# A 32-byte pad moved ahead of the attention tiles, and 64 bytes left free at the right end of SBUF, in a float32 encoder layer

## The chip, the core and the metric

One NeuronCore of a Trainium2 chip runs one launch of the kernel. The metric is the device time of that launch in microseconds (us). Engines are named as in the profile: PE (TensorE matmuls) and PEld (TensorE's weight loads), DVE (VectorE), ACT (ScalarE), POOL (GpSimd) and SP (SyncE, which issues all DMAs here). SBUF, the on-chip memory, has 128 partitions; a tile takes the same range of bytes in each of them, and an "address" below is the byte at which a tile starts within a partition.

## What is computed

One encoder layer over 2048 rows of width 1024, all in float32, cut from the reference:

```python
h = x * (1.0 + sc1) + sh1                        # sc, sh, g from the conditioning vector
proj = jnp.einsum('bsd,de->bse', h, w_in[l])     # u (512 wide) and q, k, v (512 each)
y_pool = pool_mixer(u, w_pool[l], pool_scale[l])         # means over 2/4/8/16 rows
y_attn = chunked_attention(q, k, v, rel_bias[l])         # 64-row chunks, 9-chunk band, 8 heads
y = jnp.einsum('bse,ed->bsd', jnp.concatenate([y_pool, y_attn], axis=-1), w_out[l])
x = layer_norm(ALPHA * x + (1.0 + g1) * y, ln1_g[l], ln1_b[l])
h = x * (1.0 + sc2) + sh2
f = jnp.square(jax.nn.relu(jnp.einsum('bsd,df->bsf', h, w_ff1[l])))    # 1024 -> 4096
f = jnp.einsum('bsf,fd->bsd', f, w_ff2[l])                             # 4096 -> 1024
x = layer_norm(ALPHA * x + (1.0 + g2) * f, ln2_g[l], ln2_b[l])
```

## The kernel before

Every large product is done in split float32: an operand is cut into a high part in the matmul format float32r and the rest, a low part, and three matmuls (high x high, high x low, low x high) stand for one. A matmul here has two SBUF operands: 128x128 *weights*, which are loaded first, and a *moving* operand of, mostly, 128 partitions by 512 columns of 4 bytes, which is streamed past them.

The stages, in order of time:

- **First projections** (lines 154 to 229, about 0 to 55 us): `wf` holds the weights, `hT` the modulated input, which is moving (L172).
- **Attention** (lines 231 to 750, about 55 to 640 us): `step` issues the other projections (L441, weights from `hl`, moving `hT`) a few matmuls at a time between the attention matmuls of one of 128 units: scores S (L623, weights `q`, moving `k`), transposes T of the probabilities `s` (L646) and values (L667, weights `v`, moving `PT`). DVE, ACT and POOL do the softmax and the splits.
- **Output projection** (`wout_half`, L402, weights `hl`, moving `hT`), layer norm and its transposes (L841), about 640 to 841 us.
- **Up projection** (`product`, L1067, about 841 to 1480 us): 32 turns `g`, each of seven products `s` of 12 matmuls; the weights come from `hl`, the moving operand from `hslot[s]`. The slots 0, 1, 2 and 5 are tiles of the pool `sa` (printed as `h` in the trace, `f<-h,hl`), the slots 3, 4 and 6 are tiles `sb` of the pool `big` (`f<-sb,hl`).
- **Down projection** (`f2_products` and `issue`, L1351, from about 1494 us): weights from `sa` tiles, moving `sb` tiles, 2688 matmuls, then the last layer norm.

The program's order is written out by hand: each engine runs its instructions in the order in which the code issues them, with semaphore waits between engines. What the change touches is where tiles lie. A pool takes its room in the order in which pools are opened, from the left end of SBUF upwards or, with `side="right"`, from the right end downwards, and a closed pool's room is used again by the next one. On the left stand, in this order, constants and small tiles, `stream` (`raw`, `hl`), then the first projections' pool `ada`, in its place later `attn`, and in their place, after `attnp.__exit__` at line 753, a pool `pad` of 32 bytes (lines 754 and 755) and behind it `sa` and the rest. On the right stands `big` alone: four tiles of 16384 bytes, first `hT`, later `sb` and `g`. The memset of a pad only makes the tile exist; nobody reads it.

Of the kernel before, what the change touches and what calls it, by code (L numbers as in the profile page):

```python
# [8 lines left out]
F32 = mybir.dt.float32  # L9
# [15 lines left out]
def trunk_layer(ctx: ExitStack, tc: tile.TileContext, xT, x, wada1, wada2, vecs, rows, win, wfirst, wpT, wout,  # L25
                bias, w1, w2, out):
    nc = tc.nc
# [86 lines left out]
            a_items[hf, name] = st.add(win[where[name[0]] + int(name[1])], nc.gpsimd)  # L114

    late = {}
    yi = [st.add(yS[t // 8][t % 8].rearrange("p k c -> p (k c)"), nc.vector) for t in range(16)]
    big = ctx.enter_context(tc.tile_pool(name="big", bufs=1, side="right"))
    hTs = [big.tile([128, 2, 2, 1024], F32R, name="hT", tag="big", bufs=4) for _ in range(4)]
# [24 lines left out]
    def narrow(w=512):  # L144
        return pr.tile([128, w], F32, name="pv", tag="pv", bufs=1)

    adap = tc.tile_pool(name="ada", bufs=1)
    ada = adap.__enter__()
    NF0 = len(FIRST)
# [601 lines left out]


    attnp.__exit__(None, None, None)
    padp = ctx.enter_context(tc.tile_pool(name="pad", bufs=1))
    nc.gpsimd.memset(padp.tile([128, 8], F32, name="pad"), 0.0)
    sap = ctx.enter_context(tc.tile_pool(name="sa", bufs=1))

    def slot(i, name):
# [707 lines left out]
```

## Time and profile before

| what | us |
|---|---|
| median of 3 runs | 2108.86 |
| the 3 runs | 2104.95, 2108.86, 2114.11 |
| the profiled execution, its own time | 2109.24 |
| its span, first to last instruction | 2107.5 |
| PE busy in the span | 2039.2 |
| DVE busy | 1311.7 |
| ACT busy | 1000.1 |
| POOL busy | 322.8 |

The profile is of one execution. Its timeline gives the start of a run of like instructions, the time to the end of the last one, and their count; since matmuls overlap, the time from one start to the next, divided by the count, is the pitch at which they follow each other, and this is shorter than the mean duration that a list of groups gives for one matmul.

### The profile page before, as it was taken

What the parts mean: (1) busy time and instruction counts of PE and PEld (TensorE: products, weight loads), DVE (VectorE), ACT (ScalarE), POOL (GpSimd) and SP (SyncE); (2) the same over time, 40 slices, a digit from 0 to 9 for tenths busy, and PEclk for the clock granted to TensorE, in tenths of its full rate; (3) what the DMA queues carried; (4) which work ended last, traced back from release to release, by engine and by line L of the source; (5) the groups of instructions that cost most, each with busy time, mean ns of one, the idle gap of its engine ahead of it and who ended that gap; (6) DMA issues with size and microseconds to landing.
All of it is one profiled execution on the core that took longest, in us unless ns stands there. A gap on an engine that the chain in (4) does not pass through costs nothing.

```text
span 2107.5 us, 27049 instructions
## 1 busy us (share of the span) xinstructions
PE 2039.2 (97%) x9672; PEld 1682.2 (80%) x9672; DVE 1311.7 (62%) x1974; ACT 1000.1 (47%) x1592; POOL 322.8 (15%) x426
## 2 busy tenths in 40 slices
PE   7999989999999999999999999999999999999998
PEld 6778868887877888778888788888788888888886
DVE  7555566556665464777766766666694447875448
ACT  5454555554553555545545655555453333333330
POOL 1535443553333100000000000000000001100002
PEclk9999999999999999999999999999999999999999
DMA  7444553434433678879878988887986556766552
GB/s 300 139 136 127 148 156 99 137 107 137 135 123 105 200 240 296 290 254 322 293 266 295 322 278 292 300 295 274 326 287 209 190 190 210 255 236 227 191 170 110
DMA packets 210360, 456.68 MB, mean 217 GB/s; under 512 B 18609, under 2 KB 36529, under 8 KB 209202
## 3 DMA queue, kind: packets, MB, share of 16 engines
q1 hardware_dynamic: 210226, 454.96, 64.1%
q8 instruction: 76, 1.25, 0.2%
q14 instruction: 58, 0.48, 0.1%
HBM read 294.45 MB, written 152.05 MB: 212 GB/s over the span
## 4 chain that ended last, share of the span: by engine, by line
PE 82%; DVE 7%; ACT 4%; DMA 3%; issue 2%; POOL 1%; SPq 0%; DVEq 0%; POOLq 0%; ACTq 0%
PE f L1351 26%; PE f L1067 26%; PE d L441 10%; PE d L402 7%; PE pv L667 3%; PE T L646 3%; PE S L623 2%; DVE s L630 1%; ACT PT L654 1%; PE d L172 1%; DVE PT L655 1%; PE S L172 1%; ACT s L632 1%; ACT hl L59 1%; DVE sb L60 1%
## 5 line engine op out<-in xcount | busy, mean ns | idle before, releaser
L1351 PE MATMUL f<-sb,sa 128*128 128x512 f32 x2688 | 616.3, 391 | 2.5 <-DVE sb L60 1.8
L1351 PEld LDWEIGHTS f<-sb,sa 128*128 128x128 f32 x2688 | 504.7, 188 | 114.0 <-DVE sb L60 2.5
L441 PE MATMUL d<-hT,hl 128*128 128x512 f32 x1392 | 373.2, 400 | 0.7 <-ACT vt L333 0.7
L1067 PE MATMUL f<-h,hl 128*128 128x512 f32 x1536 | 363.5, 392 | 3.5 <-ACT c L1074 2.7
L1067 PEld LDWEIGHTS f<-h,hl 128*128 128x128 f32 x1536 | 288.2, 188 | 69.7 <-ACT c L1074 4.0
L1067 PE MATMUL f<-sb,hl 128*128 128x512 f32 x1152 | 280.8, 397 | 8.0 <-ACT c L1074 5.1
L441 PEld LDWEIGHTS d<-hT,hl 128*128 128x128 f32 x1392 | 248.7, 189 | 41.0 <-ACT vt L333 1.1
L1067 PEld LDWEIGHTS f<-sb,hl 128*128 128x128 f32 x1152 | 218.5, 190 | 59.9 <-ACT c L1074 6.2
L655 DVE TENSOR_TENSOR PT<-T,PT 128x640 fp32r<-128x640 f32 (+4 forms) x128 | 94.8, 741 | 211.3 <-ACT PT L654 209.3
L632 ACT ACTIVATE s<-s,m 128x640 f32<-128x640 f32 (+4 forms) x128 | 97.9, 765 | 236.7 <-DVE m L630 182.6
L402 PE MATMUL d<-hT,hl 128*128 128x512 f32 x696 | 166.0, 395 | 0.0
L1089 ACT ACTIVATE g<-g 128x512 f32<-128x512 f32 x96 | 60.7, 633 | 213.9 <-DVE g L1080 213.9
L59 ACT CAST sb<-hl 128x1024 fp32r<-128x1024 f32 x67 | 70.2, 1048 | 178.4 <-PE f L1351 153.1
L402 PEld LDWEIGHTS d<-hT,hl 128*128 128x128 f32 x696 | 129.3, 189 | 27.0
L638 POOL TENSOR_SCALAR s<-s,m 128x640 f32<-128x640 f32 (+4 forms) x128 | 99.3, 776 | 253.2 <-DVE m L637 214.0
L60 DVE TENSOR_TENSOR hl<-wsum,hl 128x1024 fp32r<-128x1024 f32 x64 | 78.4, 1225 | 93.6 <-ACT hl L59 93.6
L60 DVE TENSOR_TENSOR sb<-hl,sb 128x1024 fp32r<-128x1024 f32 x67 | 81.9, 1222 | 68.8 <-ACT sb L59 68.5
L59 ACT CAST sb<-raw 128x1024 fp32r<-128x1024 f32 x53 | 55.3, 1052 | 119.0 <-PE f L1351 94.8
L623 PE MATMUL S<-k,q 128*128 128x320 f32 (+1 forms) x448 | 91.9, 321 | 16.6 <-DVE m L630 16.6
L623 PEld LDWEIGHTS S<-k,q 128*128 128x128 f32 x448 | 74.4, 188 | 36.3 <-DVE m L630 22.8
L1394 POOL TENSOR_SCALAR ag<-ag 128x1024 f32<-128x1024 f32 x1 | 1.0, 1047 | 665.3 <-DMA ab<-in_rows_dram 665.3
L60 DVE TENSOR_TENSOR hl<-w,hl 128x1024 fp32r<-128x1024 f32 x64 | 61.3, 957 | 63.3 <-ACT hl L59 63.3
(182 smaller groups left out, 2613.1 us busy)
## 6 DMA issues: line engine op xcount, KB each, us to landing
fS<-g SPq DMA_DIRECT2D x224, 256.0 KB, 4.2
hl<-fS SPq DMA_DIRECT2D x67, 512.0 KB, 4.6
hl<-tS SPq DMA_DIRECT2D x67, 512.0 KB, 4.9
w<-in_w_dram SPq DMA_DIRECT2D x48, 512.0 KB, 4.3
raw<-fS SPq DMA_DIRECT2D x45, 512.0 KB, 4.5
raw<-tS SPq DMA_DIRECT2D x45, 512.0 KB, 4.8
wS<-wsum SPq DMA_DIRECT2D x32, 512.0 KB, 4.8
raw<-in_w_dram SPq DMA_DIRECT2D x32, 512.0 KB, 5.1
```

The lines of the kernel that those rows point to most:

```text
L59: nc.scalar.copy(hl_h, src)
L60: low.tensor_sub(hl_l, src, hl_h.bitcast(F32))
L402: nc.tensor.matmul(ps, yc[:, a, k, :], hT(b, k, cols), start=(k == 0 and i == 0), stop=(k == 7 and i == 2))
L441: nc.tensor.matmul(ps, w[name][:, a, k, :], hT(b, k, slice(tb * 512, tb * 512 + 512)), start=(n == 0), stop=(n == 23))
L623: nc.tensor.matmul(S[:, 512 * p:512 * p + wp], q[:, i * 128:i * 128 + 128], k[:, a, k0 + p * wp:k0 + p * wp + wp], start=(a == 0), stop=(a ...
L632: nc.scalar.activation(s[:, 0:w], s[:, 0:w], AF.Exp, bias=m[:, 0:1], scale=-1.0, accum_out=m[:, 1:2])
L638: nc.gpsimd.tensor_scalar(s[:, 0:nk * 128], s[:, 0:nk * 128], m[:, 1:2], 1.0, op0=ALU.mult, op1=ALU.mult)
L646: nc.tensor.transpose(t[:, j * 128:j * 128 + 128], s[:, j * 128:j * 128 + 128], ident)
L655: nc.vector.tensor_sub(ol, src, oh.bitcast(F32))
L667: nc.tensor.matmul(pv, v[:, i + sl, h % 2, :], PTt[:, a, sl, :], start=(c == 0), stop=(c == tot - 1))
L1067: nc.tensor.matmul(ps, w[:, p, c:c + 128], h[:, q, k, :], start=first and k == 0 and (p, q) == (0, 0), stop=k == 3 and p == 1, skip_group_ ...
L1351: nc.tensor.matmul(bank, f, w, start=start, stop=stop, skip_group_check=True)
```

## The change

The pad pool is opened before `ada`, and so also before `attn`, and stays open; it is no longer opened after `attn`. A second pool of 64 bytes is opened on the right ahead of `big`.

```diff
     late = {}
+    padr = ctx.enter_context(tc.tile_pool(name="padr", bufs=1, side="right"))
+    nc.gpsimd.memset(padr.tile([128, 16], F32, name="padr"), 0.0)
...
     def narrow(w=512):
         return pr.tile([128, w], F32, name="pv", tag="pv", bufs=1)
 
+
+    pad = ctx.enter_context(tc.tile_pool(name="pad", bufs=1))
+    nc.gpsimd.memset(pad.tile([128, 8], F32, name="pad"), 0.0)
     adap = tc.tile_pool(name="ada", bufs=1)
...
     attnp.__exit__(None, None, None)
-    padp = ctx.enter_context(tc.tile_pool(name="pad", bufs=1))
-    nc.gpsimd.memset(padp.tile([128, 8], F32, name="pad"), 0.0)
     sap = ctx.enter_context(tc.tile_pool(name="sa", bufs=1))
```

The addresses that the pools then give, and what remains of them after division by 256. The slices of the matmul operands start at multiples of 512 bytes within their tiles, so a slice has its tile's remainder; where a pool holds several such tiles, all have the same one.

| tile | use | address before | remainder before | address after | remainder after |
|---|---|---|---|---|---|
| `hl` (first of 3) | weights L441, L402, L1067 | 10656 | 160 | 10656 | 160 |
| `sa` (first of 4) | moving L1067, weights L1351 | 35744 | 160 | 35744 | 160 |
| `hT`, `sb` (first of 4) | moving L172, L441, L402, L1067, L1351 | 163808 | 224 | 163744 | 160 |
| `wf` | weights L172 | 35712 | 128 | 35744 | 160 |
| `q` / `k` | weights / moving L623 | 61056 / 69248 | 128 / 128 | 61088 / 69280 | 160 / 160 |
| `v` / `PT` | weights / moving L667 | 36480 / 93824 | 128 / 128 | 36512 / 93856 | 160 / 160 |
| `xr` | DMA target, ACT and DVE operand | 129856 | 64 | 129888 | 96 |
| `xk` | DMA target, ACT and DVE operand | 93056 | 128 | 93088 | 160 |
| `raw` | DMA target, ACT and DVE operand | 2464 | 160 | 2464 | 160 |

No other instruction is added, removed or moved, on any engine, and the waits between engines are the same but for those of the pad. POOL at the start of the program, before and after (`ident` and `mhalf` are constants, the last row is the split of the first streamed weights):

```order
 masks.py:197 MEMSET ident 128x128
 masks.py:199 ISA
 masks.py:199 AFFINE_SELECT ident<-ident 128x128
 L51 MEMSET mhalf 128x1
+L118 MEMSET padr 128x16
+L151 MEMSET pad 128x8
 L60 TENSOR_TENSOR hl<-raw,hl 128x512 x4
```

Two memsets now stand between the last constant and POOL's first split. POOL at the end of attention, before:

```order
L356 TENSOR_TENSOR ws_6431<-u 128x527
L356 TENSOR_TENSOR ws_6432<-ws_6431 128x525
L638 TENSOR_SCALAR s<-s,m 128x640 x2
L755 MEMSET pad 128x8
L795 TENSOR_SCALAR mv<-mv 128x1
```

In the changed program the memset of `pad` is gone from this place, between the last softmax work and the first layer-norm work.

## Rows read from the trace of the kernel before

**Rows 1.** The page's chain that ended last, by engine and by line, shares of the span.
```profile
PE 82%; DVE 7%; ACT 4%; DMA 3%; issue 2%; POOL 1%; SPq 0%; DVEq 0%; POOLq 0%; ACTq 0%
PE f L1351 26%; PE f L1067 26%; PE d L441 10%; PE d L402 7%; PE pv L667 3%; PE T L646 3%; PE S L623 2%; DVE s L630 1%; ACT PT L654 1%; PE d L172 1%; DVE PT L655 1%; PE S L172 1%; ACT s L632 1%; ACT hl L59 1%; DVE sb L60 1%
```
**Rows 2.** Windows: PE, PEld, DVE, ACT, POOL busy (count), clock, DMA share, GB/s.
```profile
0.00:50.00 50.00, 38.19 (x183) 32.35 (x184) 37.02 (x92) 26.35 (x30) 4.38 (x10) 1.00 0.78 306
...
50.00:640.00 590.00, 559.26 (x3144) 472.13 (x3143) 342.29 (x758) 307.62 (x629) 256.42 (x322) 0.99 0.45 133
...
1000.00:1480.00 480.00, 475.66 (x2070) 387.87 (x2069) 316.61 (x399) 259.03 (x384) 0.00 (x0) 1.00 0.83 289
1500.00:2040.00 540.00, 540.00 (x2361) 443.05 (x2360) 338.56 (x324) 208.75 (x204) 16.72 (x18) 1.00 0.67 228
```
**Rows 3.** Timeline of PE, one up-projection turn: start, us to last end, count.
```profile
1209.91 8.37 PE L1067 MATMUL f<-h,hl 128*128 128x512 f32 x36
1218.12 5.67 PE L1067 MATMUL f<-sb,hl 128*128 128x512 f32 x24
1223.63 2.93 PE L1067 MATMUL f<-h,hl 128*128 128x512 f32 x12
1226.40 2.93 PE L1067 MATMUL f<-sb,hl 128*128 128x512 f32 x12
1229.16 3.16 PE L1067 MATMUL f<-h,hl 128*128 128x512 f32 x13
```
**Rows 4.** The same timeline asked from 1213.0 on: the last 24 of those 36.
```profile
1212.68 5.60 PE L1067 MATMUL f<-h,hl 128*128 128x512 f32 x24
```
**Rows 5.** PE in two windows of that turn: busy, clock, DMA share, GB/s.
```profile
1212.70:1218.10 5.40, 5.40 (x25) 1.00 0.98 356
1218.10:1223.60 5.50, 5.50 (x25) 1.00 0.82 257
```
**Rows 6.** Timeline of PE in the down projection, 1500 to 1600 us.
```profile
1499.80 100.42 PE L1351 MATMUL f<-sb,sa 128*128 128x512 f32 x438
```
**Rows 7.** Pieces of the chain that ended last (start, us): values, output projection.
```profile
379.39 1.43 PE pv L667 x12
...
702.07 11.01 PE d L402 x48
```
**Rows 8.** Timeline of PE in the first projections.
```profile
27.72 0.86 PE L172 MATMUL d<-hT,wf 128*128 128x512 f32 x3
28.42 0.39 PE L172 MATMUL pv<-hT,wf 128*128 128x512 f32 x1
28.66 0.63 PE L172 MATMUL S<-hT,wf 128*128 128x512 f32 x2
...
30.52 0.86 PE L172 MATMUL d<-hT,wf 128*128 128x512 f32 x3
```
**Rows 9.** Timeline of PE in attention.
```profile
386.08 1.55 PE L441 MATMUL d<-hT,hl 128*128 128x512 f32 x6
387.46 0.71 PE L646 MATMUL T<-ident,s 128*128 128x128 f32 x5
```
**Rows 10.** Groups by line and shape: count, busy us, mean ns of one, idle before.
```profile
L441 PE MATMUL d<-hT,hl 128*128 128x512 f32 x1392 | 373.2, 400 | 0.7 <-ACT vt L333 0.7
...
L667 PE MATMUL pv<-PT,v 128*128 128x256 f32 x672 | 97.2, 292 | 0.1
...
L623 PE MATMUL S<-k,q 128*128 128x320 f32 x384 | 74.2, 315 | 9.9 <-DVE m L630 9.8
...
L59 ACT CAST hl<-raw 128x512 fp32r<-128x512 f32 x90 | 53.5, 615 | 9.6 <-PE S L402 9.5
...
L59 ACT CAST hT<-xr 128x512 fp32r<-128x512 f32 x16 | 9.5, 615 | 0.0
```
**Rows 11.** Timeline of POOL at the start.
```profile
1.24 0.10 POOL L51 MEMSET mhalf<- 128x1 f32 x1
46.35 4.60 POOL L60 TENSOR_TENSOR hl<-raw,hl 128x512 fp32r<-128x512 f32 x3 [45.02 <-ACT hl L59]
```

## The prediction

> **What bounds the kernel now.** I read the chain that ended last first, then windows by stage, then PE's timeline inside the long stages. PE holds 82% of the chain, and its lines there are the large products, L1351 and L1067 with 26% each, L441 with 10%, L402 with 7% [rows 1]. The windows say the same by stage: PE is busy for 475.66 of 480 us in the up projection and for all of 540 in the down projection, while DVE, the next engine, has 317 and 339, and the DMA engines stand at 0.83 and 0.67 [rows 2]. So there the time is the number of matmuls times their pitch, the time from one start to the next. Nothing waits, and nothing is removed by this change; whatever it does to the total it must do through the pitch, or through the price of other operations whose tiles now lie elsewhere.
>
> The pitch is not the same everywhere, though the shape is. In one turn of the up projection the 24 matmuls from 1212.68 on take until 1218.12 us, 226.7 ns each; the next 24 take until 1223.63, 229.6 ns each [rows 3, 4]. Both runs have 512 columns, weights from `hl`, no gap, and a granted clock of 1.00, which is the 2.4 GHz level [rows 5]. DMA load doesn't explain it: the faster run is the one with more (0.98 against 0.82). What differs is the moving tile: `h` in the first, with remainder 160, which is also that of the weights; `sb` in the second, with remainder 224. The 12 matmuls after each switch from one to the other stand at 230.8 (1209.91 to 1212.68, and 1223.63 to 1226.40, both on `h`), so there is a run-in of about 4 ns times 12 after a switch [rows 3, 4].
>
> Three other stages fit. In the down projection (`sb` moving, 224; weights 160) 437 steps take 100.42 less the last matmul's 0.39 us: 228.9 ns [rows 6]. In the output projection (`hT` moving, 224; weights 160) it is 11.01 / 48 = 229.4 [rows 7]. In the first projections (moving 224, weights 128) 12 matmuls go from 27.72 to 30.52 us: 233.3 [rows 8]. Sorted by the distance of the two remainders: 0 gives 226.7, 64 gives 229, 96 gives 233.3. After the change weights and moving operand have remainder 160 in every one of these lines.
>
> **The change part by part.** It is made against the profiled execution's own 2109.24 us, 0.4 above the median of the three runs.
>
> *Up projection.* A turn takes 1229.16 - 1209.91 = 19.25 us [rows 3]. With all 84 matmuls at 226.7 ns, and no switch inside it, it takes 19.04. That is 0.21 us for each of 32 turns: 6.8 us. This combination of remainders, tiles and weights is one that the kernel runs already, so I take it whole.
>
> *Down projection.* 2688 matmuls, 228.9 - 226.7 = 2.2 ns each: 5.9 us. The remainders become those of the 226.7 run; the weights come from `sa` and not from `hl`.
>
> *Output projection.* 16 row tiles of two halves of 24 make 768 matmuls; 2.7 ns each are 2.1 us.
>
> *First projections.* 144 matmuls, 6.6 ns each: at most 0.9 us. PE is busy there for only 38 of 50 us and waits for loads and DVE [rows 2], so I take 0.5, between 0 and 0.9.
>
> *Projections inside attention.* L441 runs in pieces of five to seven between other matmuls; one piece of six takes 386.08 to 387.46 us, 230.0 each [rows 9]. At 226.7 the 1392 of them [rows 10] would save 4.6 us. But they never get past the first dozen after a switch, and the run-in above costs 4 ns on a tile with the good remainder. If a switch of line is such a switch even between equal remainders, the gain is 0. No row shows that case; I take the middle, 2.3.
>
> *Scores and values.* Weights and moving operand go from 128 and 128 to 160 and 160; the distance stays 0. The values of 256 columns stand at 1.43 / 12 = 119 ns [rows 7]. Should the remainder itself count and not the distance, the nearest price is that between 233.3 and 226.7, where one operand stood at 128: 6.6 ns for 672 values and some 450 scores [rows 10], 7.4 us, as a gain or as a loss. I take 0, since the distance orders all four pitches and the single remainder doesn't.
>
> *Other engines.* ACT's cast of 512 columns takes 615 ns from `raw` (remainder 160) and 615 from `xr` (64) [rows 10]; I take 0 for ACT, DVE and POOL. *DMA.* First loads and attention tiles are now written 32 bytes further. No row parts a transfer's time by address; 1% of the first 50 us, where the DMA share is 0.78 [rows 2], would be 0.5 us either way, and later the share leaves room. *Memsets.* Two on POOL at the start, 0.10 us each like its neighbour, in a stretch in which POOL stands idle for 45 us [rows 11]; one fewer before the first layer norm. Zero; even without that cover it would be 0.2 us.
>
> Sum: 6.8 + 5.9 + 2.1 + 0.5 + 2.3 = 17.6 us. Late next: with PE 0.8% faster, DVE and the DMA engines rise by as much from 0.66 and 0.83 in the up projection, which leaves them behind PE. 2109.2 - 17.6 = 2091.6, and 0.4 lower against the median: 2091.
>
> The Trainium skill speaks against all this. "TensorE: Matmul & The Clock Gate", in "Step-by-step: what each phase is for", gives the gap of matmuls that follow each other as columns over 2.4 GHz and a fixed 2.5 ns, 216 ns for 512 columns, with no word on addresses, and calls the two SBUF reads independent ports. By it the pitch here would be one number and the change would give nothing, 2109. The trace has neither that number nor one number (226.7, 229.6, 233.3), so I follow the rows.
>
> **The rivals.**
>
> *It isn't the remainder but the tile's region.* `sb` and `hT` lie above 163,000 bytes, `h` below 102,000; if far tiles are read at 229 and near ones at 226.7, then 64 bytes change nothing. Then only the first projections could gain, and the time is 2108 to 2109. For it: in the up projection remainder and region change together. Against it: the first projections (233.3) and the output projection (229.4) have the same moving tile, so there the weights' place decides, and weights from `sa` and from `hl`, in different regions with the same remainder, give 228.9 and 229.4. The skill's rule on the gap, above, ends at the same time.
>
> *The attention tiles get dearer.* All of them now start at an odd multiple of 32 bytes instead of an even one, and 128 units pass DVE, ACT and POOL in a chain. On the path these engines hold about 3% of the span with L630, L654, L655 and L632, some 67 us [rows 1]. Slower than before means a loss above 17.6 us, so this decides when those operations take 26% longer; at half speed it would cost 67 us, 2159 in all. The two casts at 615 ns speak against any of it.
>
> *Half of it.* The rule holds in the up projection alone, where the rows show it directly, and the weights of `sa` or the run-ins keep the rest: 2109.2 - 6.8, about 2102.
>
> **How the numbers follow.** The forecast has 0.78: 2091, and within it from 2085 (the rest of attention and first projections, 2.7, and part of the 7.4 above) to 2097 (attention 2.3 gone, and the runs' own spread, 2105 to 2114, about its middle). The region has 0.13, half of it 0.06, dearer attention 0.03. To leave out no more than 0.2 the range goes from 2084 to 2103. About 0.5%, 10.5 us, is what a measurement of this kernel can tell from no change. Faster by more needs under 2098: 0.80. Within it: 0.17. Slower: 0.03.
>
> **What would show it.** In the changed profile a turn of L1067 takes 19.04 us instead of 19.25, and the runs on `h` and `sb` have one pitch; 438 matmuls of L1351 in a row take 99.4 us and not 100.42; 48 of L402 take 10.9. L172 falls from 233.3 towards 227. The groups of ACT, DVE and POOL keep their means. If the turn stays at 19.25 with `sb` at 229.6, the region decides and the forecast is wrong; if the pitch falls but the span doesn't, something else has become late, and the windows must show idle PE in the up or down projection; if pieces of L441 stay at 230, the run-in doesn't depend on the remainder and the sum is 2.3 us too large.

## The result

The changed kernel takes 2096.45 us, the median of six runs (2093.74 to 2097.00), against 2109.77, the median of six runs of the kernel before; the ratio is 0.9927, with a 95% interval from 0.9904 to 0.9951. Run once more, beside the kernel with the right pad alone, it gave 0.9950 (0.9936 to 0.9963). The gain is thus 0.5 to 0.7%, some 11 to 13 us between the medians. The profiled execution took 2097.00 us with a span of 2095.3, so its span is 12.2 us shorter than that of the profile before.

The line numbers shift by 3 to 5: L1067 is now L1070, L1351 is L1354, L402 is L407, L441 is L446 and L172 is L177. One turn of the up projection, in PE's timeline (start, us to the last end, count; the last row is cut by the window), answers to [rows 3]:

```profile
1206.08 8.32 PE L1070 MATMUL f<-h,hl 128*128 128x512 f32 x36
1214.24 5.60 PE L1070 MATMUL f<-sb,hl 128*128 128x512 f32 x24
1219.68 2.88 PE L1070 MATMUL f<-h,hl 128*128 128x512 f32 x12
1222.40 2.88 PE L1070 MATMUL f<-sb,hl 128*128 128x512 f32 x12
1225.12 1.07 PE L1070 MATMUL f<-h,hl 128*128 128x512 f32 x4
```

The turn goes from 1206.08 to 1225.12, 19.04 us and not 19.25. The 24 matmuls on `sb` take 5.44 us, 226.7 ns each, where they took 229.6; the two runs of 12 that stood at 230.8 and 230.0 take 2.72 us, 226.7 each. The pitch no longer depends on the tile, and a switch of tile no longer costs anything. The down projection, answering to [rows 6], and the output projection as a piece of the chain, answering to [rows 7]:

```profile
1499.76 100.58 PE L1354 MATMUL f<-sb,sa 128*128 128x512 f32 x443
```
```profile
702.13 10.90 PE d L407 x48
```

(100.58 - 0.39) / 442 is 226.7 ns, where it was 228.9; 10.90 / 48 is 227.1, where it was 229.4. The windows, answering to [rows 2] (PE, PEld, DVE, ACT and POOL busy, clock, DMA share, GB/s):

```profile
50.00:640.00 590.00, 561.30 (x3143) 473.57 (x3142) 342.51 (x758) 307.89 (x629) 256.48 (x321) 0.99 0.46 132
1000.00:1480.00 480.00, 474.67 (x2081) 391.04 (x2080) 319.10 (x403) 261.80 (x386) 0.00 (x0) 1.00 0.84 292
1500.00:2040.00 540.00, 540.00 (x2384) 447.15 (x2383) 335.32 (x322) 208.62 (x204) 16.74 (x18) 1.00 0.66 226
```

In the down projection PE is as busy as it was, with 2384 matmuls in the window and not 2361. In attention the count did not move: 3143 against 3144.

Where the 12 us came from, by the starts of the first matmul of a stage in PE's timeline, of before and then of after:

```profile
633.14 0.39 PE L402 MATMUL d<-hT,hl 128*128 128x512 f32 x1
...
841.15 8.35 PE L1067 MATMUL f<-h,hl 128*128 128x512 f32 x36
...
1479.45 2.91 PE L1351 MATMUL f<-sb,sa 128*128 128x512 f32 x12
```
```profile
633.42 0.40 PE L407 MATMUL d<-hT,hl 128*128 128x512 f32 x1
...
840.14 1.07 PE L1070 MATMUL f<-h,hl 128*128 128x512 f32 x4
...
1472.64 1.52 PE L1354 MATMUL f<-sb,sa 128*128 128x512 f32 x6
```

Up to the output projection the changed kernel is 0.28 us later, the output projection gives 1.3, the up projection 638.30 - 632.50 = 5.8. From the start of the down projection to the end of the span it is 628.05 before and 622.66 after, 5.4: the pitch gives 2688 times 2.2 ns, 5.9, and 0.5 is lost at the end. Together 12.2.

### The profile page after: what moved, and what is told of

Read it like the earlier page. It is cut to its first block, busy times and chain, and to the rows that moved or that the text cites. A ratio compares the mean times of both kernels' runs of the same rounds, so it can differ in the third digit from the quotient of the medians.

```text
span 2095.3 us, 27047 instructions
## 1 busy us (share of the span) xinstructions
PE 2026.7 (97%) x9672; PEld 1682.5 (80%) x9672; DVE 1311.3 (63%) x1974; ACT 1000.4 (48%) x1592; POOL 323.1 (15%) x427
## 4 chain that ended last, share of the span: by engine, by line
PE 80%; DVE 8%; ACT 4%; DMA 3%; issue 3%; POOL 1%; SPq 0%; DVEq 0%; POOLq 0%; ACTq 0%
PE f L1354 26%; PE f L1070 24%; PE d L446 11%; PE d L407 7%; PE pv L672 3%; PE T L651 3%; PE S L628 2%; DVE s L635 1%; ACT PT L659 1%; PE d L177 1%; DVE PT L660 1%; DMA raw<-in_w_dram 1%; PE S L177 1%; ACT s L637 1%; DVE sb L60 1%
## 5 line engine op out<-in xcount | busy, mean ns | idle before, releaser
L1354 PE MATMUL f<-sb,sa 128*128 128x512 f32 x2688 | 610.3, 389 | 2.7 <-DVE sb L60 1.9
L1354 PEld LDWEIGHTS f<-sb,sa 128*128 128x128 f32 x2688 | 504.4, 188 | 108.5 <-DVE sb L60 2.7
L446 PE MATMUL d<-hT,hl 128*128 128x512 f32 x1392 | 375.0, 401 | 0.7 <-ACT vt L338 0.7
L1070 PE MATMUL f<-h,hl 128*128 128x512 f32 x1536 | 361.3, 391 | 3.4 <-ACT c L1077 2.4
L1070 PEld LDWEIGHTS f<-h,hl 128*128 128x128 f32 x1536 | 288.8, 188 | 66.4 <-ACT c L1077 3.3
L1070 PE MATMUL f<-sb,hl 128*128 128x512 f32 x1152 | 275.5, 392 | 9.5 <-ACT c L1077 4.8
L446 PEld LDWEIGHTS d<-hT,hl 128*128 128x128 f32 x1392 | 250.0, 190 | 40.8 <-ACT vt L338 1.1
L1070 PEld LDWEIGHTS f<-sb,hl 128*128 128x128 f32 x1152 | 216.9, 189 | 58.4 <-ACT c L1077 6.0
L407 PE MATMUL d<-hT,hl 128*128 128x512 f32 x696 | 165.3, 394 | 0.0
L407 PEld LDWEIGHTS d<-hT,hl 128*128 128x128 f32 x696 | 129.6, 189 | 25.8
L1323 POOL TENSOR_SCALAR zv<-zv 128x1 f32<-128x1 f32 x16 | 15.6, 974 | 549.2 <-DVE zv L1322 549.2
```

The lines of the kernel that those rows point to most:

```text
L407: nc.tensor.matmul(ps, yc[:, a, k, :], hT(b, k, cols), start=(k == 0 and i == 0), stop=(k == 7 and i == 2))
L446: nc.tensor.matmul(ps, w[name][:, a, k, :], hT(b, k, slice(tb * 512, tb * 512 + 512)), start=(n == 0), stop=(n == 23))
L1070: nc.tensor.matmul(ps, w[:, p, c:c + 128], h[:, q, k, :], start=first and k == 0 and (p, q) == (0, 0), stop=k == 3 and p == 1, skip_group_ ...
L1354: nc.tensor.matmul(bank, f, w, start=start, stop=stop, skip_group_check=True)
```

## The experiments

Two theories stood against each other at the start, beside the rivals of the forecast: that the pitch follows from how weights and moving operand lie to each other, or that a tile's own remainder or region decides. In the diffs the base is the changed kernel, unless said otherwise.

**The two pads apart.** The right pad alone, on the kernel before:

```diff
     late = {}
+    padr = ctx.enter_context(tc.tile_pool(name="padr", bufs=1, side="right"))
+    nc.gpsimd.memset(padr.tile([128, 16], F32, name="padr"), 0.0)
```

> Only the 64 bytes at the right end: hT and sb go to remainder 160, the 32-byte pad stays behind attention, so wf, q, k, v and PT stay at 128. Theory (the distance of the two remainders sets the pitch of back-to-back matmuls): nearly the whole gain stays, since L1067, L1351 and L402 then have distance 0 and a pitch of 226.7 ns; a turn of L1067 takes 19.04 us; the median is 2095 to 2098. L172 then has distance 32, which no run shows yet; between 226.7 and 229. Rival (the left pad carries a share, through attention tiles or loads): the time stands halfway, 2102 to 2106.

Measured: 0.9951 (0.9938 to 0.9964), 2098.9 us, 0.9 above the range expected. A turn of the up projection takes 19.04 us, and the down projection has the pitch of the changed kernel (443 matmuls in 100.58 us). The first projections, where the moving operand now lies 32 above the weights (160 and 128), stand at 2.80 / 12 = 233.3 ns, 28.57 to 31.37 us, above the 226.7 to 229 that I thought likely:

```profile
28.57 0.86 PE L174 MATMUL d<-hT,wf 128*128 128x512 f32 x3
29.27 0.39 PE L174 MATMUL pv<-hT,wf 128*128 128x512 f32 x1
29.50 0.63 PE L174 MATMUL S<-hT,wf 128*128 128x512 f32 x2
...
31.37 0.87 PE L174 MATMUL d<-hT,wf 128*128 128x512 f32 x3
```

The left pad alone (the changed kernel without `padr`):

> Only the 32-byte pad ahead of the first projections and attention: hT and sb stay at remainder 224, weights at 160. Theory of the distance: L1351 stays at 228.9 ns, a turn of L1067 at 19.25 us, L172 falls from 233.3 to 229 (distance 64 instead of 96), and the time is that of before within 1 us, 2108 to 2110. Rival (left pad carries a share): 2102 to 2106.

Measured: 1.0007 (0.9998 to 1.0016), 2110.91 us, 0.9 above the range expected: no gain. 438 matmuls of the down projection take 100.42 us as before, and in the first projections 12 go from 27.62 to 30.37 us, 229.2 ns, as expected for 64. So the gain is the right pad's. Since 2098.9 and 2096.45 were not taken beside each other, both kernels were run once more together:

> The changed kernel itself, on the same chip as the kernel with the right pad alone. If the left pad is worth nothing but the pitch of L172, the two medians lie within 1 us of each other, both at 2096 to 2099; if it has a share of its own, this one is 2 to 3 us faster, as the two earlier calls had it (2096.45 against 2098.9).

> The right pad alone once more, beside the changed kernel. Within 1 us of it, if the left pad is worth only the 0.5 us of L172; 2 to 3 us slower, if the left pad has a share of its own in attention.

Measured: 2096.66 us, 0.9950 (0.9936 to 0.9963), and 2096.85 us, 0.9952 (0.9940 to 0.9965). The left pad has no share in the time that these runs can show. In the traces it has two small ones that work against each other. In the first projections the mean step of the line falls from 233.5 ns to 229.3 with the left pad (`right_only`, then the changed kernel), 0.6 us over 144 matmuls. In attention the mean step from a projection matmul to the next on PE rises by 0.6 to 0.9 ns in each of the three pairs with and without it (231.0 to 231.9, 230.9 to 231.6, 231.0 to 231.6), about 1 us over the line.

**Is 160 the good remainder, or the equality?** Everything moved to remainder 0:

```diff
+    shift = ctx.enter_context(tc.tile_pool(name="shift", bufs=1))
+    nc.gpsimd.memset(shift.tile([128, 24], F32, name="shift"), 0.0)
     stream = ctx.enter_context(tc.tile_pool(name="stream", bufs=1))
...
-    nc.gpsimd.memset(padr.tile([128, 16], F32, name="padr"), 0.0)
+    nc.gpsimd.memset(padr.tile([128, 56], F32, name="padr"), 0.0)
```

> All left tiles from the streamed weights on lie 96 bytes further (24 floats ahead of the stream pool), and 224 bytes instead of 64 are left free at the right end: every matmul operand named in the table has remainder 0 instead of 160, the distance stays 0. Theory of the distance: the same as the changed kernel, 226.7 ns in L1067 and L1351, 2095 to 2098. Rival (160 itself, or an odd multiple of 32, is the good remainder of a tile): the pitch is 229 or more and the time 2108 or more.

Measured: 0.9946 (0.9932 to 0.9961), 2099.3 us, beside the 2098.9 of `right_only` and 1.3 above the range expected. A turn of the up projection takes 19.04 us. The down projection, in PE's timeline:

```profile
1499.79 100.58 PE L1356 MATMUL f<-sb,sa 128*128 128x512 f32 x443
```

The same 443 in the same 100.58 us as with remainder 160. So for these two values a tile's own remainder doesn't matter; what matters is that the two are equal. That the far tiles `sb` now run at the pitch of the near ones, here and in the changed kernel, ends the rival of the region.

**How far apart?** The free bytes at the right end set where `hT` and `sb` lie; only the size in the pad's memset line changes (32, 96, 128, 192 and 320 bytes):

```diff
-    nc.gpsimd.memset(padr.tile([128, 16], F32, name="padr"), 0.0)
+    nc.gpsimd.memset(padr.tile([128, 8], F32, name="padr"), 0.0)
```

> 32 instead of 64 bytes free at the right end: hT and sb at remainder 192, weights at 160, distance 32. If the pitch grows with the distance: between 226.7 and 229 in L1351, so 2098 to 2108. If it goes by blocks of 64 bytes in which both operands start (160 and 192 lie in different ones, 192 at its start): 229 or above, 2108 to 2112.

> 96 bytes free at the right end: hT and sb at remainder 128, weights at 160, so the moving operand lies 32 below the weights and not 32 above. Theory A (what counts is whether the two start in the same half of a 64-byte step, and then of a 128-byte step; the sign doesn't matter): as with 32 above, 233.3 ns in L1351, 2125 to 2132. Theory B (the distance upwards counts, modulo 256, here 224): a pitch that no run has shown, other than 233.3.

> 128 bytes free at the right end: hT and sb at remainder 96, weights at 160, so the moving operand lies 64 below the weights. If the sign doesn't matter, as it didn't for 32: 228.9 ns in L1351 like 64 above, 2107 to 2112. If it does: another pitch, and the only safe rule is distance 0.

> 192 bytes free at the right end: hT and sb at remainder 32, weights at 160, distance 128. Theory A (only the remainder by 128 counts, in which 0 gives 226.7, 64 gives 228.9 and odd multiples of 32 give 233.3): 226.7 ns in L1351, 2095 to 2100. Theory C (a step of 256 bytes counts): 228.9 or more, 2106 or more.

> 320 bytes free at the right end: hT and sb have remainder 160 by 256 like the weights, but lie 256 off by 512, which no run so far did. If 256 is the step after which the pattern repeats: 226.7 ns in L1351, 2094 to 2100. If the step is 512 or more: 228 to 234 ns, 2105 to 2125.

A stretch of the down projection without a wait in it, in PE's timeline, for 32, 96, 128, 192 and 320 bytes in this order:

```profile
1502.81 97.55 PE L1354 MATMUL f<-sb,sa 128*128 128x512 f32 x417 [0.75 <-DVE sb L60]
```
```profile
1499.85 100.49 PE L1354 MATMUL f<-sb,sa 128*128 128x512 f32 x430
```
```profile
1501.02 99.20 PE L1354 MATMUL f<-sb,sa 128*128 128x512 f32 x424 [0.76 <-DVE sb L60]
```
```profile
1499.85 100.33 PE L1354 MATMUL f<-sb,sa 128*128 128x512 f32 x431
```
```profile
1499.89 100.35 PE L1354 MATMUL f<-sb,sa 128*128 128x512 f32 x442
```

The pitch is the time less 0.39 us, divided by the count less one; two of the stretches begin behind a wait, where the first step is about 0.1 us longer, and that is taken off. Each of the five kernels was run once, so its time has no spread; the medians of the kernel before, taken beside them, are 2108.2 to 2111.0.

| moving less weights, remainder by 256 | where | pitch, ns | whole kernel, us |
|---|---|---|---|
| 0 | the changed kernel | 226.7 | 2096.5 |
| 0, but 256 by 512 | `pad_320` | 226.7 | 2098.0 |
| 64 | the kernel before | 228.9 | 2109.8 |
| 128 | `pad_192` | 232.4 | 2118.7 |
| 32 | `pad_32` | 233.3 | 2128.9 |
| 96 | L172 of the kernel before (pieces of 18) | 233.3 | |
| 192 (64 below) | `pad_128` | 233.3 | 2127.1 |
| 224 (32 below) | `pad_96` | 233.3 | 2125.5 |

`pad_32` was dearer than either of its expectations: 32 apart costs three times what 64 does. That the sign doesn't matter held for 32 and not for 64 (228.9 above, 233.3 below); that only the remainder by 128 counts fell with 128 at 232.4. That 256 is the step held, for distance 0. Of the seven distances seen (160 was not run, and 96 only in the short pieces of the first projections) one is best, one is second, and five cost 2.5 to 3% of the pitch; the kernel before had the second.

The same shows inside one kernel. In an up-projection turn of `pad_32`, where `sb` lies 32 from the weights and `h` still 0, the 24 matmuls on `sb` take 5.61 us, 233.8 ns each, and the 12 on `h` that follow take 2.75, 229.2 each, the run-in after the switch included:

```profile
1225.60 5.77 PE L1070 MATMUL f<-sb,hl 128*128 128x512 f32 x24
1231.21 2.92 PE L1070 MATMUL f<-h,hl 128*128 128x512 f32 x12
1233.96 2.97 PE L1070 MATMUL f<-sb,hl 128*128 128x512 f32 x12
```

**Why attention gained nothing.** The projections inside attention, in PE's timeline of the changed kernel, with the operations between their pieces:

```profile
386.18 1.40 PE L446 MATMUL d<-hT,hl 128*128 128x512 f32 x5
387.42 0.75 PE L628 MATMUL S<-k,q 128*128 128x320 f32 x4
388.01 1.56 PE L446 MATMUL d<-hT,hl 128*128 128x512 f32 x6
389.40 0.71 PE L651 MATMUL T<-ident,s 128*128 128x128 f32 x5
```

The piece of six takes 388.01 to 389.40, 231.7 ns each, though every remainder is equal now; [rows 9] had 230.0. Over the whole line the mean step of up to 250 ns from one of these matmuls to the next matmul on PE is 231.6 ns, where the kernel before had 231.0; with the right pad alone it is 230.9, so the rise goes with the left pad. To see whether the interruption is the cause, the two pieces of a unit were put together behind its scores and transposes:

```diff
-        debt += step(quota // 2 + 1, False)
+        debt += step(0, False)
...
-            debt += step(quota - quota // 2 - 1)
+            debt += step(quota)
```

> The changed kernel with the attention's interleaved projection matmuls (L441 of the kernel before) issued in one piece of eleven or twelve a unit instead of two of five to seven; all else the same. Theory (a run-in of some 24 to 40 ns after each interruption, whatever the remainders, is why attention gained nothing): the pitch of that line falls from 231.6 towards 229 ns, 3 to 4 us over 1392 matmuls, which may be lost again to waits, since scores and transposes then follow each other directly: 2090 to 2110 in all. Rival (the line is slow for another reason in attention): the pitch stays at 231 or more.

Measured: 2130.38 us, 1.0098 (1.0077 to 1.0120). A piece in its timeline, and PE's waits of this kernel and then of the changed one (in total, times, longest):

```profile
393.49 2.77 PE L446 MATMUL d<-hT,hl 128*128 128x512 f32 x11
396.10 0.74 PE L628 MATMUL S<-k,q 128*128 128x320 f32 x4
```
```profile
PE T L651 <- DVE PT L660: 33.7, 37, 1.8
```
```profile
PE T L651 <- DVE PT L660: 10.3, 14, 2.4
```

Eleven in one piece take 393.49 to 396.10, 2.61 us; five and six above take 1.24 + 1.39 = 2.63. The mean step over the line, counted as above, falls from 231.6 ns in the changed kernel to 229.5. So the pitch does depend on how long a piece is, by about the 2 ns expected, 2.6 us in all. Sorted by place in the piece (mean ns from one matmul of the line to the next, pieces beside a stretch at the lower granted clock left out), the traces show why:

| step within a piece | 1 | 2 | 3 | 4 | 5 | 6 | 7 | 8 | 9 | 10 |
|---|---|---|---|---|---|---|---|---|---|---|
| before, L441 (64 apart) | 232.3 | 232.0 | 231.0 | 229.4 | 227.0 | 230.0 | | | | |
| after, L446 (0 apart) | 231.7 | 233.3 | 230.4 | 230.9 | 230.3 | 228.2 | | | | |
| `long_pieces`, L446 (0 apart) | 231.6 | 233.5 | 231.2 | 229.8 | 230.8 | 229.1 | 227.0 | 227.5 | 227.4 | 226.7 |

The first six steps are no cheaper at distance 0 than at 64. The gain begins behind them, where the pieces of five to seven have ended. The kernel before was not run with long pieces, so what distance 64 would make of such pieces is not shown.

The order of `long_pieces` loses 34 us to the changed kernel, 29.9 of them between the first L446 and the first L407 (606.40 against 576.46 us). PE is idle there for 21.1 us more, most of it transposes that wait for DVE, and busy for 8.8 us more although the pitch fell. The granted clock is at its lower level, 1.2 GHz, for 27.3 us of this stretch and for 10.2 in the changed kernel; PE is busy for 22.8 and 9.8 us of that, so the lower level costs some 6.5 us more, by an estimate that takes half of the difference. The longest such time begins inside a wait of PE for DVE of 6.7 us (PE busy, clock, DMA share, GB/s):

```profile
309.90:320.10 10.20, 6.98 (x24) 0.50 0.47 139
```

## Why the prediction was right, and where it was off

*What bounds the kernel*, and that the change must work through the pitch of back-to-back matmuls: right. PE is as busy as it was, and the same matmuls follow each other faster. That nothing waits was too strong for the up projection: of its 638.3 us before, PE was busy for 626.8.

*Up projection.* The turn of 19.04 us came to the hundredth. The term of 6.8 measured 5.8. Turns without a wait gained 0.21 as worked out, but some wait for other engines. Over the stage, in windows of the kernel before and then of the changed one (PE, PEld, DVE, ACT and POOL busy, clock, DMA share, GB/s):

```profile
841.15:1479.45 638.30, 626.81 (x2701) 507.87 (x2700) 431.52 (x547) 338.87 (x506) 3.36 (x3) 0.99 0.83 289
```
```profile
840.14:1472.64 632.50, 619.62 (x2701) 506.89 (x2700) 430.85 (x547) 338.83 (x506) 3.35 (x3) 0.99 0.84 292
```

PE is busy for 7.2 us less and idle for 1.4 us more (11.5, then 12.9). The idle time that grew is the wait for DVE's sums, 3.6 us where it was 0.8; other waits of PE shrank by about 1.4 us together (in total, times, longest; after, then before):

```profile
PE f L1070 <- DVE g L1083: 3.6, 4, 1.7
```
```profile
PE f L1067 <- DVE g L1080: 0.8, 2, 0.6
```

Nor is all of the 7.2 us pitch. The granted clock was at 1.2 GHz for 10.2 us of this stage in the profile before and for 6.8 in the one after (PE busy, clock, DMA share, GB/s; before, then after):

```profile
855.20:862.00 6.80, 5.89 (x14) 0.50 0.91 361
903.00:906.40 3.40, 3.40 (x8) 0.50 1.01 346
```
```profile
856.10:859.50 3.40, 3.40 (x10) 0.50 1.02 413
1170.10:1173.50 3.40, 3.40 (x9) 0.50 0.99 337
```

From the steps in these rows, some 20 of about 400 to 440 ns instead of 230, I estimate the difference at 1.3 us, which leaves about 6 for the pitch. The 1.3 of the clock and the 1.4 of longer waits nearly cancel, and that is luck. The stage takes 630.9 to 633.7 us in six profiles with distance 0 and attention as it was, and 638.3 and 639.8 in the two with 64.

*Down projection.* 5.9 forecast and 5.4 measured to the end of the span, with the pitch as forecast. *Output projection.* 2.1 forecast, 1.3 measured: its first row tiles run in pieces between the last attention matmuls and the others start behind transposes, and each piece pays the run-in, which I had seen in the up projection and not counted here. The mean step of the line falls by 1.8 ns (229.3 to 227.6) and not by 2.7. *First projections.* 0.5 forecast, 0.1 measured the other way: the mean step falls from 233.3 to 229.3 ns, in pieces of 18, but the line starts 0.23 us later, behind the first load, and is 0.3 us further behind by 21 us, so the first L441 starts at 56.96 us where it was 56.86. When DVE starts on that load varies from 6.15 to 7.14 us between the profiles, without an order by the pads.

*Attention.* 2.3 forecast, as the middle between 0 and 4.6; measured 0.2 the other way, from the first L441 to the first L402. This step took about half of the difference between 17.6 and 12.2: the row I had, a run-in of a dozen matmuls, spoke for the end at 0, and I went to the middle because its switch was one between unequal remainders. The run-in follows an interruption as such. The 0.2 us is itself a sum of small terms (PE busy, clock, DMA share, GB/s; before, then after):

```profile
56.86:633.14 576.28, 548.67 (x3094) 0.99 0.45 131
```
```profile
56.96:633.42 576.46, 550.87 (x3094) 0.99 0.45 131
```

PE is idle for 2.0 us less and busy for 2.2 us more. The dearer steps of the line make some 0.8 of that. Most of the rest, by an estimate, is the granted clock: PE is busy at 1.2 GHz for 9.8 us of this stage, where it was for 6.5 before.

*Scores and values, other engines, loads, memsets.* All 0, as taken. The mean step from a values matmul to the next on PE is 127 ns in both kernels, and from a scores matmul 159, the time at 1.2 GHz left out; so moving both operands from 128 to 160 has no price there. ACT's casts, answering to [rows 10], keep their means, and so does DVE's 640-wide operation on the scores, whose tiles moved (817 ns in both kernels):

```profile
L59 ACT CAST hl<-raw 128x512 fp32r<-128x512 f32 x90 | 53.5, 615 | 9.5 <-PE S L407 9.4
...
L59 ACT CAST hT<-xr 128x512 fp32r<-128x512 f32 x16 | 9.5, 615 | 0.0
```

That removes the rival of dearer attention tiles; `left_only`, which moves all of them and the first projections' tiles and leaves `hT` and `sb`, took 1.0007 of the time.

*The rule by distance.* "0 gives 226.7, 64 gives 229, 96 gives 233.3" was read off three points as if the pitch grew with the distance. The points were right and the line through them was wrong: 32 costs as much as 96, and 128 less than either. The forecast didn't need it, since distance 0 was in the trace; a forecast for a pad of 32 bytes, made by that line, would have been 2098 to 2108 and wrong by 20 us. The rule of the Trainium skill, in "TensorE: Matmul & The Clock Gate", "Step-by-step: what each phase is for", that the gap is the columns over the clock and a constant, doesn't agree with these runs: ten kernels with the same matmuls show four pitches, none of them its 216 ns. All matmuls compared here are in float32r, so whether the format has a part in the distance from 216 ns is open.

## What to carry to other kernels

Where PE runs matmuls back to back, compare the pitch of runs with the same shape in the timeline; if it differs by tile and not by clock or load, look at the start addresses of weights and moving operand and bring them to the same remainder by 256, which one pad of 64 bytes did here. Count the matmuls that stand in long uninterrupted runs: only those gained here, and pieces of half a dozen between other work didn't. Take the price of a new distance from a run and not from a line through others: four of the pads tried here, chosen without a row for them, cost 0.5 to 0.9% against the kernel before.

## What the hardware showed that I had not expected

The pitch of 512-column float32r matmuls took four values, 226.7, 228.9, 232.4 and 233.3 ns, over seven distances, and it was not symmetric: 64 above costs 2.2 ns, 64 below 6.6. For each distance tried there it is the same within 1 ns in the up and in the down projection, under different DMA loads (shares of 0.84 and 0.66 in the changed kernel). After an interruption the first six steps stay at 228 to 234 ns even where the remainders are equal, and from the seventh on they are within 1 ns of 226.7. Why the distance counts is open. That the weight load and the moving stream get in each other's way in SBUF would fit all of this, but no run here shows it: PE's two reads were never measured apart, and with the weights of a line all at one remainder, the runs can't say whether it is the weights in use or the next ones, already being loaded, that the moving operand meets.
